# A trunk of two decoder layers: the first projection takes x with its columns first, norm weights come as columns, distance tables go between the chunks

## The chip, the cores and the metric

One core of one Trainium2 chip runs the whole program. The metric is the device time of one execution in microseconds (us), as the median of the runs shown. Engines are named as in the profile: PE is TensorE (PEld its weight loads), DVE is VectorE, ACT is ScalarE, POOL is GpSimd and SP is SyncE, which here only issues DMAs. A name with a q (SPq, ACTq) is the sequencer that issues for that engine.

## The reference

The reference is a trunk of two decoder layers on x of 512 tokens by 1024 columns, all float32. Each layer is `x = x + mixer(rms_norm(x))`, then `x = x + mlp(rms_norm(x))`. Only the beginning matters here:

```
h    = x * rsqrt(mean(x*x, columns) + eps) * g_mix[0]     # 512 x 1024
proj = h @ w_in_even                                       # 1024 x 2304: A's q, k, v; B's q, k, v
q, k = rms_norm per head of 64 columns, times their gains
A: dilated window attention with ALiBi,  B: window of 128 with sinks and ALiBi
```

The distance tables are what ALiBi and the windows need: `dist` (query position minus key position), `lt` (a logarithm of how many of A's three branches see that distance, or a very large negative number) and `lb` (B's window).

## The kernel before, in words

**Numbers in two halves.** A float32 matmul operand is split into a high part in the matmul's own rounding (F32R) and a low part, the remainder: ACT copies (`whi`, or `h` high with the norm weight as scale), DVE subtracts (`wlo`, or `h` low). Each product is then three matmuls: high x high (L231), high x low (L232), low x high (L233).

**Columns first.** The matmul contracts over partitions, so h is needed with its columns on partitions: eight chunks of 128 columns by 512 tokens. Before, x comes with tokens on partitions. In `start` (L611 to L686) each chunk is made by four PE transposes (L630) into a bank of PSUM; ACT scales it by a column of norm weights (L159, `scale_split`), DVE makes the low half (L160), and ACT copies the unscaled chunk to SBUF (L640), from where POOL's queue writes it to a DRAM buffer `xsp` (L642). The output projection of layer 0 later reads `xsp` as its residual (L475). The norm weights come as rows of 128 and are turned by a PE transpose (L624) and a DVE copy (L625) into columns of `gcol`. The rsqrt of the token norm is left out of h. It is put in later (`ecol` in the norm of the heads, L253; `rcol` in the values, L299), so `start` also sums the squares of x per token on ACT (L669), from the same token-major tiles.

**The first projection.** `qk_a(0)` (L510) is `project` (L207) over 512 columns of weights: q and k of four heads. It fills four banks, one for each 128 tokens, over eight chunks: 8 x 4 x 3 = 96 matmuls of 512 columns. Weights are loaded two chunks at a time, in two DMAs of 256 KB (L183). `norm_heads` (L240) takes the four banks: ACT copies and squares, DVE reduces and forms the rsqrt, DVE and POOL scale. Next come the values, `v_a(0)` (96 matmuls of 256 columns), and then attention heads woven with further projections by `run` (L430).

**What sets the order.** The program is written through a planner which puts the instructions of each engine into a fixed list ahead of time, by its own model of when their inputs are ready. An instruction that is ready early may so go ahead of instructions that are written before it. `keep_in_program_order`, called by `in_order` (L143) while `cnt["start"]` is set, holds an instruction behind the one written just before it on the same engine, and says nothing of any other. Every DMA counts on one of eight semaphores, taken in turn over SP's and ACT's queues together; a DMA that takes a semaphore up again waits until that semaphore's previous DMA has landed.

**The start, as it is.** `start` is a generator stepped from L537 to L550. SP's list is: the norm rows, then x in two pairs of 256 KB and one of 512 KB each, with the weights between them, then the rest of the gains (L674, L676), the sinks (L679) and `bfor` (L681). PE first runs 24 small matmuls (`WARM`, L648) on a constant. DVE runs ten operations of the distance tables (`make_tables`, L688) before it copies the norm columns, and the other nine after the first two chunks.

Of the kernel before, what the change touches and what calls it, by code (L numbers as in the profile page):

```python
# [18 lines left out]
P = 128  # L19
# [17 lines left out]
WARM = 24  # L37
# [3 lines left out]
STARTPIN = 4  # L41
JPIN = 1
PEPIN = True
XL = ((0, 0, 256), (0, 256, 512), (1, 0, 512), (1, 0, 0))
# [28 lines left out]
def trunk(ctx, tc, x, g_mix, g_mlp, w_in_even, a_q_gain, a_k_gain, b_q_gain, b_k_gain, b_sinks,  # L73
          w_out_even, w_in_odd, b_forget, c_q_gain, c_k_gain, w_out_odd, w_up, w_down, out):
# [46 lines left out]
    cnt = {"hi": 0, "start": STARTPIN}  # L121
# [69 lines left out]

    def layer_attention(li, hT, w_in, w_out, stats=None):


        with ExitStack() as c2:
# [11 lines left out]
            def project(cols, use, pat=PAT_ATT, ahead=False):  # L207
# [6 lines left out]
                for k0 in range(0, DC, kw):  # L214
# [5 lines left out]
                    if ahead:  # L220
                        yield 0
# [240 lines left out]
            def out_part(pairs, first, finish=None, tiles=None):  # L462
# [4 lines left out]
                for c in range(DC):  # L467
# [41 lines left out]
            if li == 0:  # L509
                def qk_a(g):  # L510
                    return project([(g * 256, g * 256 + 256), (512 + g * 256, 512 + g * 256 + 256)], qk_use(g, 8),
                                   *((PAT_START, True) if g == 0 else ()))
# [24 lines left out]
                tables, first, qk0 = make_tables(ap, dist, lt, lb), start(ap, hT), qk_a(0)  # L537
                next(tables)
                for i, n in enumerate((1, 1 + 8 // GRAIN, 1 + 8 // GRAIN, 1 + 8 // GRAIN)):
                    cnt["start"] = i < STARTPIN  # L540
                    next(first)
                    for _ in range(n):
                        next(qk0)
                    if i == 0:
                        next(tables)
                cnt["start"] = False
                for _ in range(8 // GRAIN):
                    next(qk0)
                next(first)
                all_of(qk0)  # L550
# [60 lines left out]
    def start(ap, hT):  # L611


        xt = [acc_slot(f"x{i}") for i in range(4)]

        def load_x(half, a, b):
            for i in range(2):
                nc.sync.dma_start(xt[2 * half + i][:, :, a:b],
# [625 lines left out]
```

## Time and profile before

| | us |
|---|---|
| median of 3 runs | 1172.7 |
| their range | 1171.73 to 1173.19 |
| the profiled execution | 1169.99 |
| its span, first to last instruction | 1168.2 |
| PE busy | 1146.4 (98%) |
| DVE busy | 879.8 (75%) |
| ACT busy | 646.6 (55%) |
| POOL busy | 203.0 (17%) |

The profile is of one execution, which the 3 runs do not contain; 1.8 us of it lie around its span. A busy time counts matmuls from their start to their modelled end, so those that overlap in the pipeline are counted as one stretch. The granted TensorE clock is 1.00 over the whole span, that is the 2.4 GHz level.

### The profile page before, as it was taken

What the parts mean: (1) busy time and instruction counts of PE and PEld (TensorE: products, weight loads), DVE (VectorE), ACT (ScalarE), POOL (GpSimd) and SP (SyncE); (2) the same over time, 40 slices, a digit from 0 to 9 for tenths busy, and PEclk for the clock granted to TensorE, in tenths of its full rate; (3) what the DMA queues carried; (4) which work ended last, traced back from release to release, by engine and by line L of the source; (5) the groups of instructions that cost most, each with busy time, mean ns of one, the idle gap of its engine ahead of it and who ended that gap; (6) DMA issues with size and microseconds to landing.
All of it is one profiled execution on the core that took longest, in us unless ns stands there. A gap on an engine that the chain in (4) does not pass through costs nothing.

```text
span 1168.2 us, 17496 instructions
## 1 busy us (share of the span) xinstructions
PE 1146.4 (98%) x6256; PEld 981.4 (84%) x6256; DVE 879.8 (75%) x1870; ACT 646.6 (55%) x1349; POOL 203.0 (17%) x296
## 2 busy tenths in 40 slices
PE   8999989999999999999999999999999999999998
PEld 7987878887988988988887888888888888888887
DVE  7878999969947847855647877788858749669676
ACT  6556867655445545444335685656756455465452
POOL 1445434200000000000155445332100000000000
PEclk9999999999999999999999999999999999999999
DMA  7532024132332332333443323343430721623403
GB/s 257 160 91 73 19 73 145 58 123 73 101 117 91 91 108 91 96 121 108 148 127 109 103 89 110 100 124 112 163 106 3 232 91 51 202 73 108 148 34 109
DMA packets 100655, 126.57 MB, mean 108 GB/s; under 512 B 6184, under 2 KB 79944, under 8 KB 100568
## 3 DMA queue, kind: packets, MB, share of 16 engines
q1 hardware_dynamic: 99384, 121.23, 34.0%
q10 hardware_dynamic: 608, 2.13, 0.5%
q0 software_dynamic: 576, 2.10, 0.4%
q8 instruction: 49, 0.80, 0.3%
q14 instruction: 38, 0.31, 0.1%
HBM read 112.29 MB, written 6.32 MB: 102 GB/s over the span
## 4 chain that ended last, share of the span: by engine, by line
PE 82%; DVE 9%; DMA 3%; ACT 2%; POOL 1%; issue 1%; SPq 0%; ACTq 0%; POOLq 0%; DVEq 0%
PE up L164 10%; PE up L167 10%; PE up L168 10%; PE pj L231 4%; PE pj L233 4%; PE pj L232 4%; PE O L382 3%; PE PT L362 2%; PE Y L1023 2%; PE Y L1022 2%; PE Y L1020 2%; PE op L168 2%; PE op L164 2%; PE op L167 2%; PE S L325 2%; DVE wlo L155 1%
## 5 line engine op out<-in xcount | busy, mean ns | idle before, releaser
L164 PE MATMUL up<-xin,whi 128*128 128x512 f32 x512 | 200.5, 392 | 0.0
L168 PE MATMUL up<-xin,whi 128*128 128x512 f32 x512 | 199.3, 389 | 0.0
L167 PE MATMUL up<-xin,wlo 128*128 128x512 f32 x512 | 199.2, 389 | 0.0
L769 ACT CAST whi<-wraw 128x512 fp32r<-128x512 f32 x228 | 139.2, 619 | 105.5 <-PE up L168 47.3
L770 DVE TENSOR_TENSOR wlo<-wraw,whi 128x512 fp32r<-128x512 f32 x228 | 151.7, 686 | 53.7 <-ACT whi L769 53.5
L168 PEld LDWEIGHTS up<-xin,whi 128*128 128x128 f32 x512 | 96.1, 188 | 20.1
L164 PEld LDWEIGHTS up<-xin,whi 128*128 128x128 f32 x512 | 96.1, 188 | 19.9 <-issue 0.2
L167 PEld LDWEIGHTS up<-xin,wlo 128*128 128x128 f32 x512 | 96.2, 188 | 19.7 <-issue 0.2
L342 ACT ACTIVATE P<-P,negm 128x128 f32<-128x128 f32 (+5 forms) x128 | 69.6, 544 | 51.8 <-DVE negm L339 47.9
L231 PE MATMUL pj<-whi,hn 128*128 128x512 f32 (+2 forms) x256 | 88.7, 346 | 0.0
L951 ACT ACTIVATE u<-up 128x512 f32<-128x512 f32 x64 | 38.3, 598 | 90.9 <-PE up L168 90.9
L233 PE MATMUL pj<-whi,hn 128*128 128x512 f32 (+2 forms) x256 | 86.9, 339 | 0.0
L232 PE MATMUL pj<-wlo,hn 128*128 128x512 f32 (+2 forms) x256 | 86.8, 339 | 0.0
L152 POOL TENSOR_SCALAR whi<-wraw 128x512 fp32r<-128x512 f32 x88 | 61.1, 696 | 141.5 <-PE pj L233 121.3
L790 DVE TENSOR_TENSOR t<-u 128x256 f32<-128x256 f32 x56 | 23.2, 424 | 63.3 <-ACT u L1094 61.5
L155 POOL TENSOR_TENSOR wlo<-wraw,whi 128x512 fp32r<-128x512 f32 x48 | 64.4, 1345 | 20.8 <-ACT whi L150 18.1
L231 PE MATMUL pj<-whi,h 128*128 128x512 f32 (+1 forms) x192 | 65.6, 348 | 0.7 <-DVE v L160 0.7
L232 PE MATMUL pj<-wlo,h 128*128 128x512 f32 (+1 forms) x192 | 65.3, 341 | 0.2 <-DVE wlo L155 0.2
L233 PE MATMUL pj<-whi,h 128*128 128x512 f32 (+1 forms) x192 | 65.5, 343 | 0.0
L350 POOL TENSOR_SCALAR P<-P,rden 128x256 f32<-128x256 f32 (+2 forms) x96 | 47.7, 500 | 90.8 <-DVE rden L345 90.1
L155 DVE TENSOR_TENSOR wlo<-wraw,whi 128x512 fp32r<-128x512 f32 (+1 forms) x72 | 49.7, 697 | 17.5 <-POOL whi L152 9.8
L374 ACT CAST PT<-PT 128x256 fp32r<-128x256 f32 (+3 forms) x128 | 49.5, 405 | 19.3 <-PE PT L362 18.5
(229 smaller groups left out, 3051.7 us busy)
## 6 DMA issues: line engine op xcount, KB each, us to landing
wraw<-in_w_up SPq DMA_DIRECT2D x64, 512.0 KB, 4.0
wraw<-in_w_down SPq DMA_DIRECT2D x56, 512.0 KB, 4.2
wraw<-in_w_in_odd SPq DMA_DIRECT2D x36, 256.0 KB, 3.4
mraw<-in_w_down SPq DMA_DIRECT2D x16, 512.0 KB, 4.7
K<-K SPq DMA_DIRECT2D x26, 256.0 KB
wraw<-in_w_in_even SPq DMA_DIRECT2D x10, 512.0 KB, 4.0
wraw<-in_w_in_even SPq DMA_DIRECT2D x16, 256.0 KB, 4.5
xl<-xsp SPq DMA_DIRECT2D x8, 512.0 KB
```

The costliest lines, as they stand in the source:

```text
L152: nc.gpsimd.tensor_scalar(dst_h, src, 1.0, 1.0, op0=OP.mult, op1=OP.mult)
L155: in_order((nc.gpsimd if lo == "pool" else nc.vector).tensor_sub(dst_l, src, dst_h.bitcast(F32)))
L164: m = nc.tensor.matmul(o, wh, xh, start=start, stop=False, skip_group_check=more)
L167: nc.tensor.matmul(o, wl, xh, start=False, stop=False, skip_group_check=more)
L168: nc.tensor.matmul(o, wh, xl, start=False, stop=stop, skip_group_check=more)
L231: nc.tensor.matmul(o, xh, hi[:, :n], start=k == 0, stop=False)
L232: nc.tensor.matmul(o, xh, lo[:, :n], start=False, stop=False)
L233: nc.tensor.matmul(o, xl, hi[:, :n], start=False, stop=k == DC - 1)
L342: nc.scalar.activation(p[:, :ne], p[:, :ne], AF.Exp, scale=-1.0, bias=negm[:, i:i + 1], accum_out=den[:, i:i + 1])
L374: nc.scalar.copy(dst[:, 0], pt[:, :n])
L769: sca(nc.scalar.copy(dst_h, src))
L770: late.append(lambda: vec(nc.vector.tensor_sub(dst_l, src, dst_h.bitcast(F32))))
```

## The change

x is given a second time with its columns first (`xt`, 1024 x 512), and all 38 columns of gains are given as one array of 128 x 38 (`gains`); both are layouts of the inputs, made before the launch. Then:

- The 32 transposes of x, the two of the gains with their DVE copies, the eight ACT copies and the four DMAs to `xsp` for layer 0 are gone. Layer 0's residual is read from `xt`.
- The first projection is written out in `start`, chunk by chunk, with the same 96 matmuls. In chunk 0 the order is all high x high, then all high x low, then all low x high; in the others the three products of one bank follow each other. Weights come in sixteen DMAs of 128 KB, and x's chunks in two of 256 KB and three of 512 KB. SP issues 22 DMAs in place of 25.
- The token-major x is still loaded for the sums of squares (`tok`), now by four DMAs on ACT's queue, written after the sinks and `bfor` behind chunk 1. The sums are written two to a chunk behind chunks 4 to 7.
- The 19 operations of the tables are spread: one behind chunk 1, two behind each of chunks 2 to 7, and the last six behind `norm_heads`.
- 36 of the small matmuls run first in place of 24.

```diff
-WARM = 24
+WARM = 36
+TABLES = (0, 1, 2, 2, 2, 2, 2, 2)
...
+    def residual(li, dp):
+        return xsp[dp] if li else xt[dp * 256:(dp + 1) * 256].rearrange("(c p) t -> p c t", p=P)
...
-                        nc.sync.dma_start(xl, xsp[c // 2])
+                        nc.sync.dma_start(xl, residual(li, c // 2))
...
+                start(ap, hT, w_in, make_tables(ap, dist, lt, lb), [bank("pA", f"pj{t}") for t in range(NT)], qk_use(0, 8))
                 all_of(v_a(0))
...
+    def start(ap, hT, w_in, tables, outs, use):
+        w = bank("pB", "warm")
         for _ in range(WARM):
             nc.tensor.matmul(w[:, :P], identb, identb, start=True, stop=True)
+        nc.sync.dma_start(gcol[:, :38], gains)
+        xs = [ap.tile([P, 2, 512], F32, tag="qk", bufs=4, name="xs") for _ in range(4)]
+        for i in range(4):
+            raw = wp.tile([P, 2, 512], F32, tag="wraw", bufs=RAW, name="wraw")
+            if i == 0:
+                nc.sync.dma_start(xs[0][:, 0], xt[:P])
+            for c in range(2):
+                k = 2 * i + c
+                for o in range(2):
+                    nc.sync.dma_start(raw[:, c, o * 256:o * 256 + 256], w_in[k * P:(k + 1) * P, o * 512:o * 512 + 256])
+                if i == 0 and c == 0:
+                    nc.sync.dma_start(xs[0][:, 1], xt[P:2 * P])
+            if i < 3:
+                nc.sync.dma_start(xs[i + 1], residual(0, i + 1))
...
+        for k in range(DC):
...
+            if k == 0:
+                in_order(nc.scalar.activation(h[:, 0, :256], src[:, :256], AF.Copy, scale=g))
+                in_order(nc.scalar.copy(hi, raw))
+                in_order(nc.scalar.activation(h[:, 0, 256:], src[:, 256:], AF.Copy, scale=g))
+                in_order(nc.vector.tensor_sub(lo, raw, hi.bitcast(F32)))
+                in_order(nc.vector.scalar_tensor_tensor(h[:, 1], src, g, h[:, 0].bitcast(F32), op0=OP.mult, op1=OP.subtract))
+            else:
+                scale_split(h[:, 0], h[:, 1], src, g)
+                split(hi, lo, raw, "act")
...
+                nc.tensor.matmul(outs[t], h[:, part, t * P:(t + 1) * P], wt, start=k == 0 and i == 0,
+                                 stop=k == DC - 1 and i == 2)
+            for _ in range(TABLES[k]):
+                next(tables)
+            if k == 1:
+                nc.scalar.dma_start(sink, bass.AP(tensor=b_sinks.tensor, ...))
+                nc.scalar.dma_start(bfor, bass.AP(tensor=b_forget.tensor, ...))
+                for i in range(4):
+                    in_order(nc.scalar.dma_start(tok[i], x[0, i % 2 * 256:i % 2 * 256 + 256, i // 2 * 512:i // 2 * 512 + 512]
+                                                 .rearrange("(t p) d -> p t d", p=P)))
+            if k >= 4:
+                i = k - 4
+                for t in range(2):
+                    junk = ap.tile([P, 512], F32, tag="sq", bufs=1, name="junk")
+                    in_order(nc.scalar.activation(junk, tok[i][:, t], AF.Square,
+                                                  accum_out=ms[:, i // 2, i % 2 * 2 + t:i % 2 * 2 + t + 1]))
+        cnt["start"] = False
...
+        use(outs)
+        for _ in tables:
+            pass
```

## Rows read from the trace of the kernel before

**Rows 1.** The page: the span, the busy time of each engine, and the chain that ended last, by engine.

```profile
span 1168.2 us, 17496 instructions
PE 1146.4 (98%) x6256; PEld 981.4 (84%) x6256; DVE 879.8 (75%) x1870; ACT 646.6 (55%) x1349; POOL 203.0 (17%) x296
...
PE 82%; DVE 9%; DMA 3%; ACT 2%; POOL 1%; issue 1%; SPq 0%; ACTq 0%; POOLq 0%; DVEq 0%
```

**Rows 2.** The waits of PE in the first 80 us: in total, times, longest.

```profile
PE xT L630 <- DMA x<-in_x: 1.9, 2, 1.6
PE pj L231 <- DVE v L160: 0.7, 1, 0.7
```

**Rows 3.** The timeline of PE: start, busy us, instruction. Four rows are from 2 to 10 us, four show the later transposes among the products, and the last two are the end of the first projection and the first matmul of the values.

```profile
2.05 2.74 PE L648 MATMUL warm<-identb 128*128 128x128 bf16 x24 [2.05 <-DVE identb L98]
4.72 0.28 PE L624 MATMUL pg<-ident,rows 16*128 16x16 f32 x1
...
9.25 0.88 PE L630 MATMUL xT<-ident,x 128*128 128x128 f32 x6 [0.28 <-DMA x<-in_x]
9.88 0.48 PE L231 MATMUL pj<-whi,h 128*128 128x512 f32 x1
...
15.43 1.03 PE L630 MATMUL xT<-ident,x 128*128 128x128 f32 x8
16.22 1.17 PE L231 MATMUL pj<-whi,h 128*128 128x512 f32 x4
17.55 0.50 PE L232 MATMUL pj<-wlo,h 128*128 128x512 f32 x1 [0.16 <-DVE wlo L155]
...
24.51 0.39 PE L231 MATMUL pj<-whi,h 128*128 128x512 f32 x1
...
33.81 0.39 PE L233 MATMUL pj<-whi,h 128*128 128x512 f32 x1
...
34.29 0.38 PE L231 MATMUL pj<-whi,h 128*128 128x256 f32 x1
```

**Rows 4.** The timeline of SP, which issues DMAs (start, us, DMA, count), and two of SP's waits in the first 80 us.

```profile
3.19 0.98 SPq L618 DMA_DIRECT2D x<-in_x  x2
...
SPq L676 <- DMA x<-in_x: 1.4, 2, 0.8
...
SPq L676 <- DMA wraw<-in_w_in_even: 0.9, 4, 0.4
```

**Rows 5.** Stretches of the start: from and to in us, length, busy time (and instructions) of PE, PEld, DVE, ACT and POOL, granted clock, busy share of the DMA engines, GB/s moved.

```profile
0.00:5.00 5.00, 2.95 (x26) 2.72 (x26) 3.12 (x8) 1.49 (x2) 1.88 (x10) 1.00 0.49 140
5.00:10.00 5.00, 3.10 (x18) 2.46 (x18) 4.04 (x9) 2.20 (x5) 0.00 (x0) 1.00 1.01 307
10.00:15.00 5.00, 5.00 (x25) 4.12 (x24) 4.83 (x11) 3.26 (x7) 0.78 (x1) 1.00 1.06 366
```

**Rows 6.** Groups of ACT and of DVE in the first 30 us: line, engine, operation, out<-in, shape, count, busy us, mean ns of one, idle before.

```profile
L150 ACT CAST whi<-wraw 128x512 fp32r<-128x512 f32 x11 | 6.6, 642 | 0.0
L669 ACT ACTIVATE junk<-x 128x512 f32<-128x512 f32 x8 | 5.2, 656 | 0.1
L159 ACT ACTIVATE h<-xT,gcol 128x512 fp32r<-128x512 f32 x8 | 5.1, 696 | 5.6 <-DVE gcol L625 5.6
...
L669 ACT ACTIVATION_READ_ACCUMULATOR junk<-x 128x1 f32 x7 | 1.5, 209 | 0.0
...
L155 DVE TENSOR_TENSOR wlo<-wraw,whi 128x512 fp32r<-128x512 f32 x10 | 6.5, 684 | 1.5 <-ACT whi L150 1.5
L160 DVE SCALAR_TENSOR_TENSOR h<-xT,gcol,h 128x512 fp32r<-128x512 f32 x8 | 5.6, 745 | 3.7 <-ACT h L159 3.7
L306 DVE SCALAR_TENSOR_TENSOR bias<-dist,lt 128x512 f32<-128x512 f16 x2 | 1.4, 684 | 0.0
```

**Rows 7.** The timeline of DVE: the tables' last operations with the bias of a first head (L306) among them, and a scaling of the values after the projection.

```profile
12.57 0.43 DVE L710 TENSOR_SCALAR mi<-lt 128x512 f32<-128x512 f32 x1
13.03 0.69 DVE L711 TENSOR_TENSOR f<-f,mi 128x512 f32<-128x512 f32 x1
13.75 0.43 DVE L712 COPY lt<-f 128x512 f32<-128x512 f32 x1
14.22 0.29 DVE L713 TENSOR_SCALAR f<-dist 128x256 f32<-128x256 f16 x1
14.43 0.22 DVE L714 TENSOR_SCALAR lb<-dist 128x256 bf16<-128x256 f16 x1
14.56 0.69 DVE L306 SCALAR_TENSOR_TENSOR bias<-dist,lt 128x512 f32<-128x512 f16 x1
15.16 0.42 DVE L715 TENSOR_TENSOR lb<-lb,f 128x256 bf16<-128x256 bf16 x1
...
47.43 0.47 DVE L160 SCALAR_TENSOR_TENSOR v<-pj,rcol,v 128x256 fp32r<-128x256 f32 x1
```

**Rows 8.** From the timelines of ACT, POOL and PE: the copy of the first bank (L247) that begins the norm of the heads, POOL's scaling of q and k, and the first transpose that needs it.

```profile
30.61 0.61 ACT L247 COPY qk<-pj 128x512 f32<-128x512 f32 x1
...
42.85 2.95 POOL L260 TENSOR_TENSOR qk<-qk,rs 128x512 f32<-128x512 f32 x2 [0.41 <-issue]
...
46.98 0.27 PE L267 MATMUL qkT<-ident,qk 128*128 128x128 f32 x1
```

More of the change, by code (lines that the diff above doesn't have):

```diff
@@ L119, in trunk @@
     ecol = consts.tile([P, NT], F32, name="ecol")
[L121 removed]
+    cnt = {"hi": 0, "start": False}
     def rsqrt_small(dst, v):
@@ L609, in token_sums @@
         return pc[:, :NT]
[L611 to L618, printed above, removed]
-                                  x[0, i * 256:(i + 1) * 256, half * 512 + a:half * 512 + b]
-                                  .rearrange("(t p) d -> p t d", p=P))
-        def gains(rows, n, o):
-            pg = bank("pA", "pg")
-            nc.tensor.transpose(pg[:, :n], rows[:n, :], ident[:n, :n])
-            in_order(nc.vector.tensor_copy(gcol[:, o:o + n], pg[:, :n]))
-        def chunk(c):
-            pt = bank("pB", "xT")
-            for t in range(NT):
-                m = nc.tensor.transpose(pt[:, t * P:(t + 1) * P],
-                                        xt[c // 4 * 2 + t // 2][:, t % 2, (c % 4) * P:(c % 4 + 1) * P], ident)
-                if PEPIN:
-                    in_order(m)
-            h = slot(f"h0_{c}")
-            scale_split(h[:, 0], h[:, 1], pt, gcol[:, c:c + 1])
-            hT.append(h)
-            def spill():
-                if c % 2 == 0:
-                    xs.append(ap.tile([P, 2, 512], F32, tag="qk", bufs=4, name="xs"))
-                nc.scalar.copy(xs[-1][:, c % 2], pt)
-                if c % 2:
-                    nc.gpsimd.dma_start(xsp[c // 2], xs[-1])
-            return spill
-        w = bank("pA", "warm")
@@ new lines, in start @@
+        ms = small.tile([P, 2, NT], F32, tag="ms0", name="ms0")
+        tok = [acc_slot(f"x{i}") for i in range(4)]
+        sink = small.tile([P, HA], F32, tag="sink", name="sink")
+        cnt["start"] = True
+        for k in range(DC):
+            g = gcol[:, k:k + 1]
+            src = xs[k // 2][:, k % 2]
+            h = slot(f"h0_{k}")
+            hT.append(h)
+            hi = wp.tile([P, 512], F32R, tag="whi", bufs=NHI, name="whi")
+            lo = wp.tile([P, 512], F32R, tag="wlo", bufs=NLO, name="wlo")
+            raw = raws[k // 2][:, k % 2]
+            if k == 0:
[7 more added lines that the diff above has]
+                split(hi, lo, raw, "act")
+            products = ((0, hi), (0, lo), (1, hi))
+            for n, (t, i) in enumerate([(t, i) for i in range(3) for t in range(NT)] if k == 0 else
+                                       [(t, i) for t in range(NT) for i in range(3)]):
+                part, wt = products[i]
+                nc.tensor.matmul(outs[t], h[:, part, t * P:(t + 1) * P], wt, start=k == 0 and i == 0,
[3 more added lines that the diff above has]
+            if k == 1:
+                nc.scalar.dma_start(sink, bass.AP(tensor=b_sinks.tensor, offset=b_sinks.offset, ap=[[0, P], [1, HA]]))
+                nc.scalar.dma_start(bfor, bass.AP(tensor=b_forget.tensor, offset=b_forget.offset, ap=[[0, P], [1, HC]]))
+                for i in range(4):
[4 more added lines that the diff above has]
+                for t in range(2):
+                    junk = ap.tile([P, 512], F32, tag="sq", bufs=1, name="junk")
+                    in_order(nc.scalar.activation(junk, tok[i][:, t], AF.Square,
+                                                  accum_out=ms[:, i // 2, i % 2 * 2 + t:i % 2 * 2 + t + 1]))
@@ L1233 @@
     arrays, args = {}, []
-    for name in _INS:
-        a = np.ascontiguousarray(inputs[name])
+    inputs = {k: np.asarray(v) for k, v in inputs.items()}
+    for name, a in [(n, inputs[n]) for n in _INS] + list(layouts(inputs).items()):
+        a = np.ascontiguousarray(a)
         arrays[f"in_{name}"] = a
```

81 lines of the change are left out of this document (23 added, 58 removed).

## The prediction, made before the changed kernel ran

> **What bounds the kernel now.** I read the page first [rows 1]: PE is busy 98% of the span and holds 82% of the chain that ended last, at the full granted clock. So a gain must be PE time saved, or PE made to start its work earlier; both hold to the end only if PE stays the engine that is last everywhere behind. Then PE's waits [rows 2]: in the first 80 us they come to a few us, 1.9 of them on x. The timeline of PE [rows 3] shows where its real work starts. It runs small matmuls, turns x, and its first product stands at 9.88, right behind transposes that waited for x until 9.25. The projection's last product is at 33.81, and the values begin at 34.29. Between, products follow each other every (33.81 - 24.51) / 41 = 0.227 us, so 96 take 21.8 us. The rest of 34.29 - 9.88 = 24.4 us is two blocks of eight transposes, 16.22 - 15.43 = 0.8 us each, a late `wlo` at 17.55 (0.4 us more than the pitch gives), the transpose of gains and slower products around these. The stretch to judge is thus 0 to 34.29. The change is worth 34.29 less the time at which the values begin after it, plus or minus what DVE does with that behind it.
>
> **What PE is spared.** All transposes among the products (1.6 us), the wait at 17.55 and the transpose of gains go, 2.6 us together with the slower products. Transposes ahead of 9.88 only filled waiting time. What PE then does is 21.8 us of products from its first one on, plus new waits. Twelve more small matmuls cost (4.72 - 2.05) / 24 = 0.111 us each [rows 3]: the 36 end at 6.05. I cost them at nothing, covered by the loads; 6.05 is the earliest start of the first product.
>
> **Which loads come first.** This decides the rest. The four loads `tok` are written behind chunk 1, but each is only held behind the instruction written before it on ACT, and for the first that is the load of `bfor`, which is held behind nothing, like the sinks before it. They need no other result. The trace shows what the planner does with work that is ready early: L306, a head's bias, is written behind the whole value projection and ran at 14.56, between two operations of its own tables [rows 7]. So I expect all six loads of ACT's queue at the front, in the first us, sharing the DMA engines with the loads that chunks 0 to 2 wait for.
>
> **When the chunks land.** Loads moved 140 GB/s over the first 5 us (0.70 MB), then 307, then 366 [rows 5]. The slower stretch has x and weights in rows of 1 KB, the faster one x in rows of 2 KB; after the change three quarters of the early bytes have 2 KB, so I take 366 from 2.7 us on (5 - 0.70 / 0.307). The other end is 307. Landing is later than moving: the second pair of x completes 1.5 MB asked for and ended PE's wait at 9.25, while 1.5 MB had moved by 5 + 0.80 / 0.307 = 7.6, so 1.6 us. When both queues have work I give each half. Own bytes and `tok` bytes: chunk 0 needs 0.52 MB with 0.26 of `tok` (ACT's queue begins with two small loads), chunk 1 1.03 + 0.77, chunk 2 1.8 + 1.55, since x's chunks 2 and 3 are one load. They land at 6.4, 9.2 and 13.5.
>
> **From landing to product.** ACT scales (0.70) and casts (0.64), DVE subtracts (0.68) [rows 6].
> - Chunk 0: half a scale, then the cast, 1.0 us: first product at 7.4. Its twelve products end at 10.1; their lows are ready in time in the new order.
> - Chunk 1: scale and cast end at 10.5, `wlo` at 11.2, which the second product needs; the other eleven end at 13.7. PE waits 1.0 us.
> - Chunk 2: 14.8 and 15.5, end 18.0; a wait of 1.6 us.
> - Chunk 3 has landed long before 18.0 (another 0.25 MB, then the rest of `tok`), and so has each later one: 4 MB for the projection and 2 MB of `tok` at 366 are through by 2.7 + 16.4 + 1.6 = 20.7. Five chunks of 2.72 us end at 31.6.
>
> The values begin at 31.7, 2.6 us earlier. Without sharing, chunk 0 would land at 5.7 and start at 6.7, nothing waits, and the values begin at 28.6: 5.7 us earlier. At 307 GB/s with sharing, they begin at about 32.6: 1.7 us. These are the ends.
>
> **ACT and DVE beside the products.** ACT spends 1.34 us on a chunk, and from chunk 4 on two squares with their reads, 2 x (0.66 + 0.21) = 1.7 us [rows 6]; 3.1 us against PE's 2.72, for four chunks. ACT is ahead by then: chunk 4 lands by 17 and is due at 20.7, so the 1.5 us which it loses are covered; without that lead they would cost PE those 1.5 us. DVE spends 0.75 + 0.68 and two table operations of 0.43 and 0.69 at most: 2.5 us, within 2.72. The issue of a DMA takes SP 0.49 us [rows 4]; 22 take SP to 11.5 us, ahead of what chunks need. Six on ACT fall into its idle time before 6 us. SP waits in turn for a landing before it can reuse a semaphore: L676 waited four times for weights and twice for x, each issued eight DMAs earlier [rows 4]. With eight in flight I see no stall longer than the loads' own.
>
> **Behind the projection.** Three things move onto DVE's path there. Six table operations (L710, L711, L712, L713, L714, L715) are written behind the norm of the heads: 0.43 + 0.69 + 0.43 + 0.29 + 0.22 + 0.42 = 2.5 us. Two biases ran at 0.68 each before the projection ended [rows 6]; they need these tables: 1.4 us. And the banks end later relative to the end: L247 could start at 30.61, 3.7 us before 34.29 [rows 3, 8], while after the change the first bank is complete 9 products, 2.0 us, before it: 1.6 us less overlap. Against that stand the statistics and the values' splits, which get done while PE is still at chunks 6 and 7, and slack: POOL finished q and k at 45.8, and the first transpose that uses them ran at 46.98 [rows 8], 1.2 us later. With loads in by 20.7, DVE has some 4 us free before the values begin, so the tables can go there as L306 did. I take no loss, and the 0.7 us that PE waited for the values' L160 [rows 2, 7] as gone, since DVE was late there. The ends are a loss of 2.5 + 1.4 + 1.6 - 1.2 = 4.3 us and a gain of 0.7. The residual read from `xt` is the same number of loads, long before they are needed, and the DMAs to `xsp` were on no path: nothing.
>
> **Sum.** 2.6 + 0.7 = 3.3 us off the profiled execution's 1169.99, 1166.7. That execution is 2.7 us under the median of the runs shown, so on their scale 1172.7 - 3.3 = 1169.4.
>
> **A rule against it.** The weights now come in loads of 128 KB in place of 256 KB; the trace has no such loads, so I took the rate of its 256 KB ones, 366 at best [rows 5]. The Trainium skill, page DMA: Bandwidth & Descriptors, section Bandwidth, states that loads should be batched to 1 MiB or more, with 138 GB/s at 64 KB and 341 at 1 MB, measured one at a time. If I estimate 200 GB/s for 128 KB from that page, chunk 2 lands about 1 us later and the time is 1170.4. The trace speaks against it: 256 KB loads with eight in flight already moved more than the page's figure for 1 MB.
>
> **Rivals.**
> - *The loads of `tok` do not get in the way*: they go out late, behind chunk 1, without holding ACT, or the queues do not share evenly. For it: that is where they are written. Against it: L306. The values begin at 28.6 to 30: 1166.3 to 1168.
> - *ACT is held behind chunk 1*: the loads stay there, and each waits for the landing of one eight earlier, as SP did [rows 4], with chunk 2's scale behind them on ACT. The last would wait for chunk 6's weights: about 3.8 MB and 0.3 of `tok`, landed at 15.5. Chunk 2 then has its `wlo` at 17.9 against 12.1 due, and the values begin at 34.1: 1172.5, no change.
> - *DVE becomes the bound behind the projection*: tables and biases come ahead of the scaling of q and k, PE reaches L267 and waits. The price is 4.3 us; it decides once more than 1.2 us of that work is put in front. With the forecast's projection that gives 1174.4, with the one that starts late 1175.3 to 1176.8, as the statistics are late as well. For it: they are written there; DVE is busy to nine tenths in that stretch before. Against it: the planner filled gaps with L306.
> - *No change at all*, because the list of the whole program is planned anew and PE loses elsewhere what it gains: 1172 to 1173.5.
>
> **Numbers.** About 0.2% (2.4 us) can be told from no change. Chances: forecast 0.46 (its own range 1168.2 to 1171.2), unhindered loads 0.20, ACT held 0.17, DVE 0.11, planned anew 0.06. Faster takes three quarters of the forecast's and all of the second: 0.55. Slower is DVE's and a little of the last: 0.12. The rest, 0.33, is within 0.2%. The range reaches from unhindered loads, 1166.4, to 1173.6, past ACT held and the first part of DVE's case.
>
> **What would show it.** Right: ACT's four loads of x issued before 5 us; first product near 7.4; waits of PE of one to two us ahead of chunks 1 and 2 and none later; the values near 31.7; no wait at L231 behind them, and PE's waits after 80 us unchanged in sum. Wrong: a first product at or after 9; ACT's loads after 8 us; a wait at L267 or at the first scores; new waits late in the kernel; or values before 30.

## The result, and the profile after

The changed kernel is slower: a median of 1178.28 us (4 runs, 1177.30 to 1178.79) against 1172.68 us of the kernel before beside it (4 runs), a ratio of 1.0048 with a 95% interval of 1.0033 to 1.0063. The forecast was 1169.4 us, and 1178.3 lies outside its range. The profiled execution took 1177.30 us with a span of 1175.5, at a granted clock of 1.00 like the one before: 7.3 us between the two profiled spans, 5.6 between the medians. The profiled execution of the kernel before was 2.7 us under its median and this one 1.0 under its own, so up to 1.7 us of what the two traces show apart may lie in these two executions.

Six marks on PE, read from its timeline, say where these 7.3 us lie (us from the span's start):

| mark | before | after | lost since the mark above |
|---|---|---|---|
| first product of the first projection | 9.88 | 10.27 | 0.4 |
| first matmul of the values | 34.29 | 36.14 | 1.5 |
| first transpose of q and k | 46.98 | 52.2 | 3.4 |
| first matmul of the output projection | 159.3 | 164.3 | -0.2 |
| first matmul of the first MLP | 227.8 | 234.5 | 1.7 |
| end of the span | 1168.2 | 1175.5 | 0.5 |

So nothing was won at the front, 3.4 us were lost right behind the projection, and 1.7 us in a stretch where the change touches nothing but the load of the residual. PE's waits of the first 85 us show the first and the second of these; they answer to [rows 2].

```profile
PE pj L644 <- ACT whi L633: 10.3, 1, 10.3
PE pj L229 <- ACT sq L247: 1.8, 1, 1.8
PE pj L229 <- DVE v L156: 1.5, 2, 1.0
```

The reader should see that the wait for the values' scaling has not gone (0.7 before, 1.5 now), and that a new one for the squares of the heads stands beside it. PE's timeline at the front answers to [rows 3]:

```profile
10.27 2.08 PE L644 MATMUL pj<-whi,h 128*128 128x512 f32 x4 [10.27 <-ACT whi L633]
12.14 1.06 PE L644 MATMUL pj<-wlo,h 128*128 128x512 f32 x2
13.07 2.77 PE L601 MATMUL warm<-identb 128*128 128x128 bf16 x36
15.64 0.71 PE L644 MATMUL pj<-wlo,h 128*128 128x512 f32 x2
...
36.14 0.28 PE L229 MATMUL pj<-whi,h 128*128 128x256 f32 x1
```

The 36 small matmuls ran among the products and held them for 15.64 - 13.07 = 2.6 us. The stretches of the start (columns as in [rows 5]), with two single us in between, show what the loads moved:

```profile
0.00:5.00 5.00, 0.00 (x0) 0.00 (x0) 0.33 (x2) 1.49 (x2) 2.06 (x11) 1.00 0.40 48
5.00:10.00 5.00, 0.00 (x0) 0.00 (x0) 0.00 (x0) 0.91 (x2) 0.00 (x0) 1.00 0.88 312
...
2.00:3.00 1.00, 0.00 (x0) 0.00 (x0) 0.00 (x0) 0.67 (x2) 0.42 (x1) 1.00 0.72 57
3.00:4.00 1.00, 0.00 (x0) 0.00 (x0) 0.16 (x1) 0.00 (x0) 0.18 (x1) 1.00 0.80 57
```

48 GB/s over the first 5 us, where the kernel before moved 140, and from 2 to 4 us the DMA engines are 72% to 80% busy while they move 57 GB/s. What was on them is in the list of DMA issues of the first 10 us (count, KB each, median us to landing):

```profile
gcol<-in_gains SPq DMA_DIRECT2D x1, 19.0 KB, 2.8
sink<-in_b_sinks ACTq DMA_DIRECT2D x1, 4.0 KB, 3.0
bfor<-in_b_forget ACTq DMA_DIRECT2D x1, 8.0 KB, 6.3
```

These are 128 rows each of 152, 32 and 64 bytes; the rows of `sink` and `bfor` all read the same short row of their input. The timeline of ACT has the issues of its queue and the two instructions in front of the first product, and SP's has an issue that took 2.12 us, against 0.49 in [rows 4]:

```profile
0.74 0.41 ACTq L649 DMA_DIRECT2D sink<-in_b_sinks  x1
1.25 0.39 ACTq L650 DMA_DIRECT2D bfor<-in_b_forget  x1
1.66 0.46 ACTq L652 DMA_DIRECT2D x<-in_x  x1
7.27 0.51 ACT L632 ACTIVATE h<-xs,gcol 128x256 fp32r<-128x256 f32 x1 [4.60 <-DMA xs<-in_xt]
9.60 0.62 ACT L633 CAST whi<-wraw 128x512 fp32r<-128x512 f32 x1 [1.82 <-DMA wraw<-in_w_in_even]
11.04 0.45 ACTq L652 DMA_DIRECT2D x<-in_x  x1
11.52 1.50 ACTq L652 DMA_DIRECT2D x<-in_x  x2
...
2.60 2.12 SPq L616 DMA_DIRECT2D xs<-in_xt  x1
```

Only one of the four loads of `x` went to the front; three stayed behind chunk 1's cast. SP waited for these loads to land before it could use their semaphores again, 6.0 us in three waits where [rows 4] have 1.4 in two:

```profile
SPq L614 <- DMA x<-in_x: 6.0, 3, 4.3
```

Behind the projection, DVE's and ACT's timelines (they answer to [rows 7] and [rows 8]) hang together:

```profile
12.79 0.22 DVE L94 CAST identb<-ident 128x128 bf16<-128x128 f32 x1
...
35.93 0.42 DVE L702 COPY lt<-f 128x512 f32<-128x512 f32 x1
37.29 0.68 DVE L248 TENSOR_REDUCE ss<-sq 128x8 f32<-128x512 f32 x1
37.96 0.42 DVE L708 TENSOR_TENSOR lb<-lb,f 128x256 bf16<-128x256 bf16 x1
39.77 0.69 DVE L304 SCALAR_TENSOR_TENSOR bias<-dist,lt 128x512 f32<-128x512 f16 x1
...
38.00 0.60 ACT L247 ACTIVATE sq<-pj 128x512 f32<-128x512 f32 x1 [1.65 <-DVE ss L248]
```

The second square of the heads waits on ACT for DVE's first reduction, since `sq` has one buffer; that reduction came at 37.29, behind tables, statistics and splits on DVE; and PE waits for the square, since it frees the bank that the values need. The last table copy stood at 13.75 before [rows 7] and stands at 35.93 now.

### The profile page after: what moved, and what is told of

It is laid out like the page before. It is cut to its first block, busy times and chain, and to the rows that moved or that the text cites. A ratio compares the mean times of both kernels' runs of the same rounds, so it can differ in the third digit from the quotient of the medians.

```text
span 1175.5 us, 17431 instructions
## 1 busy us (share of the span) xinstructions
PE 1143.1 (97%) x6234; PEld 978.2 (83%) x6234; DVE 879.3 (75%) x1868; ACT 644.0 (55%) x1342; POOL 200.1 (17%) x292
## 4 chain that ended last, share of the span: by engine, by line
PE 83%; DVE 8%; DMA 4%; ACT 2%; issue 1%; POOL 1%; SPq 0%; ACTq 0%; POOLq 0%
PE up L160 10%; PE up L163 10%; PE up L164 10%; PE pj L229 4%; PE pj L231 4%; PE pj L230 4%; PE O L380 3%; PE PT L360 2%; PE Y L1016 2%; PE Y L1015 2%; PE Y L1013 2%; PE op L164 2%; PE op L160 2%; PE op L163 2%; DMA wraw<-in_w_in_even 2%; PE S L323 1%
## 5 line engine op out<-in xcount | busy, mean ns | idle before, releaser
L231 PE MATMUL pj<-whi,hn 128*128 128x512 f32 (+2 forms) x256 | 86.9, 339 | 0.0
L151 POOL TENSOR_TENSOR wlo<-wraw,whi 128x512 fp32r<-128x512 f32 x48 | 64.0, 1336 | 21.5 <-ACT whi L146 18.7
L151 DVE TENSOR_TENSOR wlo<-wraw,whi 128x512 fp32r<-128x512 f32 (+1 forms) x71 | 49.7, 702 | 17.5 <-POOL whi L148 9.4
L337 DVE CUSTOM_DVE_ANT_0 P<-S,bias 128x128 f32<-128x128 f32 (+1 forms) x96 | 45.9, 484 | 16.5 <-PE S L326 11.2
L229 PE MATMUL pj<-whi,h 128*128 128x256 f32 (+1 forms) x160 | 54.1, 339 | 3.3 <-ACT sq L247 1.8
L762 ACT CAST whi<-mraw 128x512 fp32r<-128x512 f32 x64 | 38.8, 619 | 33.1 <-DVE mraw L873 14.4
```

The lines of the kernel that those rows point to most:

```text
L151: in_order((nc.gpsimd if lo == "pool" else nc.vector).tensor_sub(dst_l, src, dst_h.bitcast(F32)))
L229: nc.tensor.matmul(o, xh, hi[:, :n], start=k == 0, stop=False)
L231: nc.tensor.matmul(o, xl, hi[:, :n], start=False, stop=k == DC - 1)
L762: sca(nc.scalar.copy(dst_h, src))
```

## Experiments

All ratios are against runs of the kernel before on the same chip, with their 95% interval; e5 to e8 ran on a second chip and e9 to e12 on a third, so a difference between ratios of two of these groups holds a difference of chips too. The marks come from each run's own profiled execution, in us; "values" is their first matmul, which in e1, e6 and e8 itself waited for a square (0.9, 0.5 and 1.3 us); "heads" is the first transpose of q and k, less the beginning of the values; "op to MLP" is the stretch from the output projection to the MLP. The rows stand in the order in which the kernels ran.

| run | ratio to before | first product | values | heads | op to MLP |
|---|---|---|---|---|---|
| before | 1 | 9.88 | 34.29 | 12.7 | 68.5 |
| after | 1.0048 (1.0033 to 1.0063) | 10.27 | 36.14 | 16.1 | 70.2 |
| e1_no_small | 1.0036 (1.0023 to 1.0049) | 10.25 | 34.73 | 16.0 | 69.9 |
| e2_hold | 1.0068 (1.0054 to 1.0082) | 6.47 | 35.01 | 15.0 | 70.2 |
| e3_small_late | 1.0025 (1.0017 to 1.0034) | 6.98 | 33.49 | 15.2 | 70.4 |
| e4_both | 1.0087 (1.0073 to 1.0101) | 6.36 | 39.54 | 15.1 | 70.2 |
| e5_tables_early | 1.0030 (1.0018 to 1.0042) | 10.39 | 36.84 | 13.4 | 70.1 |
| e6_late_early | 1.0010 (1.0001 to 1.0018) | 7.27 | 33.69 | 14.5 | 70.2 |
| e7_all_three | 1.0038 (1.0025 to 1.0051) | 7.36 | 32.11 | 15.6 | 70.4 |
| e8_late_first | 1.0028 (1.0018 to 1.0037) | 7.10 | 33.08 | 15.9 | 70.1 |
| e9_last_two | 1.0031 (1.0020 to 1.0042) | 10.29 | 36.60 | 13.7 | 70.2 |
| e10_late_early_two | 0.9995 (0.9986 to 1.0004) | 7.39 | 33.38 | 13.2 | 70.3 |
| e11_all_four | 1.0006 (0.9997 to 1.0015) | 7.19 | 32.49 | 17.5 | 69.7 |
| e12_inputs | 1.0024 (1.0013 to 1.0035) | 8.68 | 34.76 | 15.0 | 70.3 |
| e13_before_shift | 1.0007 (0.9998 to 1.0015) | 10.33 | 35.34 | 12.7 | 70.3 |
| e14_no_small | 1.0011 (1.0002 to 1.0020) | 7.16 | 32.48 | 16.2 | 69.7 |
| e15_more_first | 0.9990 (0.9981 to 0.9999) | 7.12 | 33.91 | 13.2 | 69.7 |
| e16_one_third | 0.9988 (0.9980 to 0.9997) | 7.41 | 32.10 | 14.3 | 69.9 |

**The small matmuls and ACT's loads.** Three runs: without the small matmuls, with ACT's six loads held where they are written, and with these held and the small matmuls first.

```diff
-WARM = 36                                  # e1
+WARM = 0
-nc.scalar.dma_start(sink, ...)             # e2, e4; bfor likewise
+in_order(nc.scalar.dma_start(sink, ...))
-nc.vector.memset(ones, 1.0)                # e4; the product gg likewise
+tc.keep_in_program_order(nc.vector.memset(ones, 1.0))
```

> The 36 small matmuls are left out; all else as in the changed kernel. In its trace they stand between products from 13.07 to 15.64 us. Theory 1 (the order on PE costs the time): PE has all it needs for the next products, so the values begin 2.6 us earlier, at 33.5, and the end follows by 2 to 2.6: 1175.7 to 1176.3. Theory 2 (late loads, and through them the late squares and tables on ACT and DVE, set the norm of the heads): the values may begin earlier, but the first transpose of q and k stays within 0.8 us of 52.2 and the time stays at 1177.5 to 1178.5; the wait of the values' matmuls for the heads' squares grows from 1.8 to some 4 us. Theory 3 (the small matmuls lifted the pace of the products from 0.43 to 0.23 us): without them the products go on at 0.43 for some us, and the values begin less than 1.5 us earlier.

> The loads of the sinks and of b_forget are held in the written order like the four loads of x behind them, so that all six stand behind chunk 1's cast on ACT; the small matmuls stay where the planner puts them. Theory 2 (loads): chunk 0's weights land near 6 us in place of 9.5, the first product is at 6.5 to 7.5 in place of 10.27; chunk 2 may wait for ACT, which issues loads that wait for earlier landings, until 11 to 13 us. Values at 32 to 34 in place of 36.1; time 1174 to 1176. Theory 1 (the order on PE): the small matmuls still stand in the middle and cost 2.6; the first product is earlier, but the time falls by less than 2 us, 1176.5 to 1178.5.

> The loads held as in e2_hold, and the small matmuls first: the constant which they use is made first on DVE, and the product of gains that waited for a load at the head of DVE's list is held in its written place. If loads and PE's order are the two causes, the effects add: first product at 6.5 to 7.5, no small matmuls among the products, values at 29.5 to 31.5, time 1169 to 1172, as forecast for the change itself. If the tables and the late norm behind the projection cost the time by themselves, values begin early and PE waits for the heads' squares and for q and k, and the time stays above 1174.

e1: the last product of the projection began 2.5 us earlier, at 33.46 in place of 35.91, so nearly all of the hold came out. But the values began only 1.4 us earlier, since their first matmul then waited for a square of the heads:

```profile
33.46 0.39 PE L644 MATMUL pj<-whi,h 128*128 128x512 f32 x1
34.73 0.39 PE L229 MATMUL pj<-whi,h 128*128 128x256 f32 x1 [0.88 <-ACT sq L247]
```

The first thirteen products are slow with and without the small matmuls: 4.6 us in e1, 4.5 in the changed kernel with the hold taken off, 3.0 at the pitch of the rest. From the values to the heads it stayed at 16.0 us, and the ratio fell by 0.0012, less than the intervals are wide. The rest of the gain went around the heads and behind them: PE waited 3.4 us for the values' scaling in place of 1.5, and after that the granted clock fell.

```profile
PE pj L229 <- DVE v L156: 3.4, 2, 2.0
...
50.00:60.00 10.00, 8.27 (x48) 7.92 (x49) 5.29 (x8) 2.52 (x4) 4.12 (x5) 0.66 0.33 82
```

From the heads to the output projection e1 took 115.0 us, the changed kernel 112.1. The one execution of e1 with a mean granted clock of 1.000 took 1174.38 us, the four at 0.995 to 0.997 took 1177.06 to 1178.22.

e2: with the small loads gone from the front the first product stood at 6.47 and the first transpose of q and k 2.2 us earlier than in the changed kernel, and yet its ratio is higher. As in e1 the granted clock read 0.66 from 50 to 60 us, behind waits of 3.0 us for the values' scaling, and 114.7 us passed from the heads to the output projection. At the front ACT's four loads took it 9 us, and chunk 2's scale came behind them:

```profile
8.22 8.98 ACTq L652 DMA_DIRECT2D x<-in_x  x4
17.25 0.72 ACT L155 ACTIVATE h<-xs,gcol 128x512 fp32r<-128x512 f32 x1 [9.29 <-DMA x<-in_x]
```

In e2 the small matmuls stood in that hole and PE waited 1.4 us; in e4 nothing filled it. PE waited 8.9 us, and the granted clock, 1.00 until then, stood at 0.51 and 0.50, near its 1.2 GHz level, in the stretches from 15 and from 20 us:

```profile
10.00:15.00 5.00, 2.12 (x10) 1.42 (x8) 0.00 (x0) 0.00 (x0) 0.00 (x0) 1.00 0.82 256
15.00:20.00 5.00, 0.00 (x0) 0.00 (x0) 0.00 (x0) 0.22 (x1) 0.20 (x1) 0.51 0.93 302
20.00:25.00 5.00, 3.94 (x9) 3.14 (x10) 4.43 (x9) 4.97 (x11) 0.00 (x0) 0.50 0.92 322
```

So the rival "ACT is held behind chunk 1" names a real cost, and it is not what made the changed kernel slow: there, most of it did not happen.

**The small loads.** `sink` and `bfor` go to the end of SP's first loads; the first load of `tok` stays free to go to the front.

```diff
-nc.scalar.dma_start(sink, ...)             # bfor likewise
+nc.sync.dma_start(sink, ...)
-    in_order(nc.scalar.dma_start(tok[i], ...))
+    m = nc.scalar.dma_start(tok[i], ...)
+    if i:
+        in_order(m)
```

> The two small loads (sinks, b_forget) go on SP behind the 22 loads of the projection; the first load of x stays at the front of ACT's queue. It tells small loads from large ones: in the changed kernel the DMA engines were 72 to 80% busy at 57 GB/s from 2 to 4 us. If the rows of 32 and 64 bytes hold the engines, the first 5 us move 0.55 MB or more in place of 0.24, and the first product comes at 8 to 9 in place of 10.27. If it is the sharing with the 512 KB of x, or the gains' rows of 152 bytes, the first product stays within 0.6 us of 10.27. Time: 1176 to 1177.5 in the first case, 1178 in the second.

The first product moved from 10.27 to 6.98 and the values from 36.14 to 33.49; the first 5 us moved 186 GB/s in place of 48, with a load of `tok` at the front as in the changed kernel, and the time fell by 0.23% (2.7 us by the ratios). The two small loads, not the shared queues, held the front; nor did the gains' rows of 152 bytes, which stayed at the front here. Whether it is the shortness of the rows or that all 128 read the same one, no run separates.

**The tables.** Ten table operations ahead of chunk 0 and nine behind chunks 1 to 3 (e5); six and thirteen on top of e3 (e6).

```diff
-TABLES = (0, 1, 2, 2, 2, 2, 2, 2)
+EARLY = 10                                 # e6: 6
+TABLES = (0, 3, 3, 3, 0, 0, 0, 0)          # e6: (0, 3, 3, 3, 4, 0, 0, 0)
...
+        for _ in range(EARLY):
+            next(tables)
         for k in range(DC):
```

> The changed kernel with one thing undone: ten of the distance tables' operations stand ahead of chunk 0 on VectorE, where it is idle from 3.8 to 9.7 us, and the other nine behind chunks 1 to 3. Nothing else moves. Theory: tables that run behind the projection hold the statistics and the values' casts on VectorE. First product (10.3 us) and beginning of the values (36.1 us) stay within 0.5 us; from there to the first transposes of the heads it falls from 16.1 us to 12.7 to 13.5 (12.7 in the kernel before), and the time from 1178.3 to 1174.8 to 1175.8 us. Rival: ScalarE sets that stretch (squares of x and squares of the heads): it stays at 14.5 to 16 us and the time at 1177 to 1178.3 us.

> The kernel with the small loads at the end of SP's list (1175.3 us), and the tables early besides: six operations ahead of chunk 0, the rest behind chunks 1 to 4. Theory of the tables: values begin at 33.5 us as there, from there to the first transposes of the heads 12.7 to 13.3 us instead of 15.2, time 1172.3 to 1173.5 us. Rival (ScalarE sets it, or what is won is waited for again behind it): 1174.7 to 1175.5 us.

e5 has the result of the theory: from the values to the heads 13.4 us in place of 16.1, and in PE's waits the squares fell from 1.8 to 0.4 us:

```profile
PE pj L230 <- DVE v L157: 1.1, 1, 1.1
...
PE pj L230 <- ACT sq L248: 0.4, 1, 0.4
```

e6 shows that this isn't all: with a faster front 1.6 us of waiting for squares came back. Its time fell by 0.15% under e3.

**The banks.** Chunks 6 and 7 are multiplied together, token tile by token tile, so that a bank is complete every 1.36 us.

```diff
-            for n, (t, i) in enumerate(...):
+            held.append((k, h, ((0, hi), (0, lo), (1, hi))))
+            if k >= DC - 2 and k < DC - 1:
+                order = []
...
+                order = [(c, t, i) for t in range(NT) for c in range(len(held)) for i in range(3)]
```

> The changed kernel, and only the products of chunks 6 and 7 taken together, token tile by token tile (six products for each of the four tiles), so that the four PSUM banks are done 1.36 us apart instead of 0.68; in the kernel before they were 2.7 us apart. Theory: the wait of the values for ScalarE's squares of the heads (1.8 us) comes from four banks that are done together; it falls under 0.5 us, and the time by 1 to 1.8 us, to 1176.5 to 1177.3. Rival: VectorE's tables set the end of that stretch anyway (they are still late here): the wait goes and 16 us from the values to the transposes stay, time within 0.5 us of 1178.3.

> Small loads late, tables early (1172.0 us), and chunks 6 and 7 token tile by token tile besides. With the tables out of the way the theory of the banks expects the wait for the squares (1.6 us) gone, 12.7 to 13.2 us from the values to the transposes instead of 14.5, and the time down by 1 to 1.5 us: level with the kernel before or under it by up to 1 us. Rival: the wait turns into one for VectorE's reductions; time within 0.4 us of the kernel without it.

e9, with the tables still late, has 0.3 us of waiting for squares in place of 1.8, 13.7 us to the heads and 0.17% less time; the rival (no gain while the tables are late) is out. In e10 all waits at L231 come to 0.5 us, the transposes of q and k begin at 46.6 (46.98 before), and the kernel is level with the kernel before.

**The small matmuls first.** They read the tile of ones, which is ready at 1 us, in place of the identity.

```diff
-nc.tensor.matmul(w[:, :P], identb, identb, start=True, stop=True)
+nc.tensor.matmul(w[:, :P], ones.bitcast(BF16)[:, :P], ones.bitcast(BF16)[:, :P], start=True, stop=True)
```

> Small loads late, and the 36 small matmuls ahead of the products by the tile of ones; the tables stay late. Theory: the 2.8 us that they held among the products go: values begin at 31 instead of 33.5 us and the time falls from 1175.3 to 1172.5 to 1173.5 us. Rival: chunks 2 to 4 come so late from the loads that the products wait for them instead, or VectorE behind the projection takes it back: values at 32.5 to 33.5 us or a longer stretch behind them, 1174.5 to 1176 us.

> Small loads late, tables early, and the 36 small matmuls read the tile of ones (seen as bf16), so that they stand ahead of the products on TensorE and not among them. Theory of three separate terms: values begin at 31 us, 12.7 to 13.3 us from there to the transposes, time 1169.5 to 1171.5 us, below the kernel before (1172.7 us) by 1 to 3 us. Rival (what is won at the front comes back as a wait or as a lower clock, as it did with no small matmuls at all): 1173 to 1175 us.

> Small loads late, tables early, chunks 6 and 7 together, and the small matmuls first, by the tile of ones, 60 of them instead of 36, so that they reach from 2 us to the first product at 7.3 us. Theory: without the 2.3 us of waiting between them and the products the granted clock stays at its upper level in every run, and all terms add up: values begin at 31 to 32 us, transposes 13 us behind, time 2 to 4 us under the kernel before. Rival (the front is bound by the landings of chunks 1 to 4, not by the small matmuls): values at 33 us, time level with the kernel before.

All three missed. In e7 and e8 PE stood idle for 2.3 and 2.4 us between the last small matmul and the first product. In e8's trace the granted clock then read 0.66 from 7 to 12 us; e7's execution at a mean granted clock of 1.000 took 1172.23 us, three at 0.994 took 1176.4 to 1177.5. In e11 60 small matmuls reached up to the products, and the first four ran in 8.23 - 7.19 = 1.04 us, against 12.14 - 10.27 = 1.87 in the changed kernel:

```profile
1.06 5.97 PE L603 MATMUL warm<-ones 128*128 128x128 bf16 x60 [1.06 <-DVE ones L98]
7.19 1.21 PE L654 MATMUL pj<-whi,h 128*128 128x512 f32 x4 [0.16 <-ACT whi L638]
8.23 1.08 PE L654 MATMUL pj<-wlo,h 128*128 128x512 f32 x4
```

Products that were ready early bought little: e11's PE waited 2.8 us for squares and 17.5 us passed to the heads.

**Where inputs lie.** All seventeen inputs of the kernel before are declared, in its order, and the two new ones behind them.

```diff
-for name, a in [(n, inputs[n]) for n in _INS] + list(layouts(inputs).items()):
+for name, a in [(n, inputs[n]) for n in order] + list(layouts(inputs).items()):
...
+    if name in _INS or name in ("xt", "gains"):
         args.append(t)
```

> The changed kernel with all seventeen inputs declared in the order of the kernel before (the eight that it doesn't read among them), the two new ones behind them, and no other edit: the order of every engine's work stays. In all kernels with the change the weights of the output projection land 1.2 us later than in the kernel before and that projection up to the first product of the MLP takes 70 us instead of 68.5. If where the inputs lie in memory makes that: 68.5 to 69 us, time 1176.5 to 1177 us. If not: 70 us and 1178.3 us, and the cause stays open.

The stretch it was meant for stayed at 70.3 us, so its theory is out there. But the front moved: `bfor` landed after 4.6 us in place of 6.3, the first product stood at 8.68, and the time fell by 0.24%. So what the small loads cost changed with which inputs are declared, and in what order; how, no run here shows.

```profile
bfor<-in_b_forget ACTq DMA_DIRECT2D x1, 8.0 KB, 4.6
```

**The output projection.** Every engine has the same order there in the kernels compared (before, changed, e10, e13 and e15), yet the changed ones take 1.1 to 1.9 us longer. In the changed kernel, ACT's cast of the projection's weights waits, and PE behind it:

```profile
181.19 0.62 ACT L146 CAST whi<-wraw 128x512 fp32r<-128x512 f32 x1 [1.33 <-DMA wraw<-in_w_out_even]
...
182.73 0.38 PE L380 MATMUL O<-PT,v 128*128 128x256 f32 x1 [0.88 <-ACT PT L372]
```

The DMA queues of 178.2 to 179.2 us (packets, MB, share of 16 engines' time) show a guest among the weights' packets, a 16 KB packet of instructions that holds one of sixteen engines for 0.9 us:

```profile
q1 hardware_dynamic: 197, 0.19, 60.5%
q8 instruction: 1, 0.02, 5.8%
```

It passes 14 us behind the start of this projection; in the kernel before it passed at 7 us, ahead of the bursts. The change leaves PE another number of instructions ahead of this point, so the fetch falls elsewhere. e13 shifts the kernel before by 48 instructions, e15 shifts e10 by 48 the other way, and e14 and e16 have fewer small matmuls.

```diff
-WARM = 24                                  # e13, the kernel before
+WARM = 0
-WARM = 36                                  # e14: 0; e16: 12
+WARM = 0
+for _ in range(24):                        # e15, ahead of the 36
+    nc.tensor.matmul(w[:, :P], ones.bitcast(BF16)[:, :P], ones.bitcast(BF16)[:, :P], start=True, stop=True)
```

> The kernel before, with its 24 small matmuls left out (they write a bank that nobody reads), so that TensorE's instructions come 48 places earlier in its stream. In the kernel before the 16 KB packet that fetches instructions passes 7 us behind the beginning of the output projection, between two bursts of loads; in the changed kernel it passes 14 us behind it, inside the burst that brings the projection's weights, and one cast waits 1.3 us. Theory of the fetch: here too it comes at 13 to 15 us, a cast waits 0.9 to 1.4 us for the weights, and the stretch from that projection to the first product of the MLP becomes 69.5 to 70.3 us (68.5 before). Rival (the stretch is longer for another reason, such as the load of the residual from the new input): 68.5 us stays.

> Small loads late, tables early, chunks 6 and 7 together, the 36 small matmuls as there, and 24 more on the tile of ones ahead of the first product, where TensorE is idle: 48 instructions more in its stream. Theory of the fetch: it passes at 7 us behind the beginning of the output projection, the cast's wait for weights (1.5 us) falls to 0.3 us or less and that stretch from 70.3 to 69.0 to 69.8 us; values as there (33.4 us); time 1169.5 to 1170.5 us. Rival: 70.3 us stays and so does the time, 1171 us.

> Small loads late, tables early, chunks 6 and 7 together (1171.0 us), and no small matmuls at all (they held the products for 3.3 us). Theory of separate terms: first product at 7.4 us, values begin at 30.3 to 31.5 us, time 1167.5 to 1169.5 us, under the kernel before by 2 us or more. Rival: the products then reach the late chunks and ScalarE's copies sooner than these are ready, and PE waits there or runs at a lower granted clock, as when the small matmuls alone were left out of the changed kernel (1.4 us of 2.8 came through): 1170.5 to 1172.5 us.

> Small loads late, tables early, chunks 6 and 7 together, and 12 small matmuls instead of 36. Theory of separate terms: the hold among the products falls from 3.3 to 1.1 us, values begin at 31.2 to 32 us; the fetch of instructions, 48 places on, passes at 17 to 19 us behind the beginning of the output projection and so behind the burst; time 1168 to 1170 us. Rival: the 2.2 us are waited for behind it (chunks 2 to 4, ScalarE's copies): 1170.5 to 1172 us.

e13 brought the loss into the kernel before: the packet at 14 us, 70.3 us in place of 68.5, and the same wait:

```profile
177.00 0.62 ACT L150 CAST whi<-wraw 128x512 fp32r<-128x512 f32 x1 [1.48 <-DMA wraw<-in_w_out_even]
```

In e15 the packet is back at 7 us and that cast's wait is 0.21 us, but the stretch fell only to 69.7: PE now waits 0.6 us longer for DVE's maxima (L339). The rows of DVE and POOL show why (the first two are from the kernel before, the others from e15):

```profile
177.65 0.69 DVE L155 TENSOR_TENSOR wlo<-wraw,whi 128x512 fp32r<-128x512 f32 x1
177.76 3.43 POOL L155 TENSOR_TENSOR wlo<-wraw,whi 128x512 fp32r<-128x512 f32 x2
...
177.62 2.96 POOL L153 TENSOR_TENSOR wlo<-wraw,whi 128x512 fp32r<-128x512 f32 x2
177.69 1.76 DVE L153 TENSOR_TENSOR wlo<-wraw,whi 128x512 fp32r<-128x512 f32 x1
```

Before, DVE's subtraction begins 0.11 us ahead of POOL's and takes 0.69 us, and POOL's two take 3.43; in e15 POOL's begin 0.07 us ahead and take 2.96, and DVE's takes 1.76, with the maxima behind it. e14 and e16 have the same (1.77 on DVE); e13 and the changed kernel, where POOL also begins first, have 1.26. So two things lie in these 1.8 us: the packet, which made some 0.6 in the changed kernels (70.3 to 69.7), and which of the two engines begins its subtraction first. e13 shows that a shift of PE's instructions alone brings both into the kernel before; it does not show the share of each. And e13's time is only 0.07% above the kernel before, with 1 inside the interval, though its profiled span is 2.6 us longer: the 1.8 us are read from single executions.

e16 holds the products for 1.3 us with its small matmuls and is, with e15, 0.1% under the kernel before, both intervals just below 1; e14, with none, is 0.1% above it. The squares are one reason: in e14 as in e11 the second one waits 1.6 us for DVE's reduction, and PE waited 2.8 us for squares, in e16 0.9.

## Why the prediction was wrong

- **"I cost them at nothing, covered by the loads; 6.05 is the earliest start."** This step failed first. The small matmuls need the identity from DVE, DVE's list had it behind chunk 1's lows, at 12.79, and they ran among the products. The hold was 2.6 us in the row above, and without them (e1) the last product of the projection began 2.5 us earlier. The same step of the prediction took 0.227 us for every product from the first one on; the first thirteen took 4.5 us besides the hold, not 3.0, another 1.5 us that it had at nothing.
- **"I take 366 from 2.7 us on."** The loads' sharing was argued at length and the two small loads were called "small" and given no time. They set the front: first product at 10.27 in place of 7.4. With them late it stood at 6.98 (e3), so the rest of that step was sound to 0.4 us. But the six loads didn't come together at the front, and the waits of 1.0 and 1.6 us ahead of chunks 1 and 2 did not come; nor did they in e14, with the first product at 7.16 and no small matmuls.
- **"I take no loss", behind the projection.** It measured 3.4 us, inside the bounds that the text gave (a loss of 4.3), and the ingredients were the ones listed: late tables, biases, banks done close together. What failed is the choice between the ends. DVE's free time before the values was counted on, from loads that are through by 20.7 (its 4 and 2 MB are 4.19 and 2.10, which gives 21.5). DVE did stand free, 6.5 us ahead of chunk 0 and 4.5 in gaps behind it, but the tables were not put there. And "no stall longer than the loads' own" failed: SP's 6.0 us of waiting put chunk 4's cast at 21.47, and the last squares of `x` began at 30.64. Nor was the place right: not a wait at L267, but banks that ACT and DVE free late. e5 and e9 each give back 2.4 to 2.7 us of that stretch, and together with a fast front (e10) nearly all of it.
- **"PE's waits after 80 us unchanged."** They grew, from 11.8 to 14.2 us in sum. 0.9 of this is the wait behind the late cast, and that mechanism was on no list: the fetch of PE's instructions moved into a burst of loads. Another 0.9 is a longer wait for K's loads, which no run explains. The Trainium skill, page Runtime: NRT & Kernel Launch, section Instruction fetch mechanics, says that each engine's stream is refilled in blocks of 16 KiB and that the cost is mostly hidden. The trace agrees on the size (49 packets, 0.80 MB), and the changed kernel and e13 show a case in which it is not hidden: a cast waits 1.3 and 1.5 us for its weights, 0.2 in e15 and e16, where the packet passes elsewhere.
- **The rule weighed against the change** gave 1170.4 by slower 128 KB loads. It is not what happened: in e12, with the same 128 KB loads among those of x, 5 to 10 us moved 374 GB/s. The prediction's "measured one at a time" is its own reading: the Trainium skill, page DMA: Bandwidth & Descriptors, section Bandwidth, gives its figures by the size of a load and does not say how many were in flight. Where the small loads were in flight the trace has 57 GB/s at 72% to 80% busy, against 366 at full share [rows 5]. The Trainium skill, page DMA: Bandwidth & Descriptors, section Why small descriptors are slow (HBM only), says that each descriptor carries a fixed overhead that weighs most on short ones. The trace agrees in direction for the rows of 32 and 64 bytes, though not for the gains' 152, which held nothing in e3. The prediction did not look at row lengths of the loads it called small.

Of the rivals, DVE's (slower, 1174.4 to 1176.8) came nearest, with a chance of 0.11. It and the forecast both missed the front.

## What to carry to other kernels

Work that "is ready early" runs where the engine that makes its input has it in its list; look there before it is costed at nothing. At the head of a queue, a load of few bytes can be dear: look at how its rows are read. When an edit frees one engine, ask which single buffer or bank the next engine has to give back first: here each term alone gave a third to a half, and only small loads late, tables early and banks spread together brought the change level with what it replaced.

## What was not expected of the hardware

- With two loads of 4 and 8 KB in flight, 128 times the same row of 32 or 64 bytes, the DMA engines were 72% to 80% busy for 2 us at 57 GB/s; `bfor` took 6.3 us to land, or 4.6 with other inputs declared around it.
- Where a 16 KB packet of instructions ran in a burst of loads, a cast waited 1.3 to 1.5 us for weights, and 0.2 where it ran elsewhere; it moved when 48 instructions were added or taken away some 150 us earlier.
- Of two subtractions that ran together on DVE and POOL, the one that began second was the slower: DVE's took 1.76 us begun 0.07 us behind POOL's, 0.69 begun 0.11 us ahead.
- The first products ran at 0.43 to 0.47 us each after idle time, though the granted clock reads 1.00 there, and at 0.26 right behind small matmuls; the later ones take 0.227.
- Where PE waited for 8.9 us (e4), the granted clock read 0.51 and 0.50 from 15 to 25 us; behind two waits of 3.4 us together (e1) it read 0.66 from 50 to 60 us, and behind waits of 1.5 us (the changed kernel) it stayed at 1.00.
